# Spreading a background gather: fewer steps in the latents' first mixer, more in the last third of the first expert pass

## The chip, the cores and the metric

The kernel runs on one core of one Trainium2 chip. The metric is the device time of one execution in microseconds. The core has five engines that matter here: TensorE (PE, with weight loads as PEld), VectorE (DVE), ScalarE (ACT), GpSimd (POOL), and SyncE (SP), which issues most transfers. [...]

## The reference

Two layers of a diffusion backbone over 512 latent tokens (width 1024), with 256 context tokens beside them. Each layer is a mixer (windowed attention with context keys, pooling, a gated chunk mixer, joined by gates and an output projection) and then a retrieval of single-neuron experts. The context is updated only in the first layer. The part that the change touches is the expert retrieval:

```python
def peer_ffn(h, w_q, subkeys, u_tab, v_tab):          # one block of 128 tokens at a time
    q = (xb @ w_q).reshape(PEER_BLOCK, PEER_HEADS, 2, PEER_HALF)
    s = jnp.einsum("thpd,hpkd->thpk", q, subkeys)
    sv, si = lax.top_k(s, PEER_TOPK)
    ...                                                 # 16 of the 256 sums, for each of 8 heads
    experts = jnp.take_along_axis(cand_e, top_pos, axis=-1)
    gate = jax.nn.softmax(top_s, axis=-1)
    act = jax.nn.gelu(jnp.einsum("td,thkd->thk", xb, u_tab[experts]))
    return jnp.einsum("thk,thkd->td", (gate * act), v_tab[experts])

for layer in range(2):
    x = x + gt1 * merge_branches(...)                   # mixer of the latents
    if not last: xc = xc + cgt1 * merge_branches(...)   # mixer of the context
    x = x + gt2 * peer_ffn(modulate(x), ...)
    if not last: xc = xc + cgt2 * peer_ffn(modulate(xc), ...)
return rms_norm(x, g_final)
```

Every token has 128 experts (8 heads of 16) out of 16384, each with a row of 1024 numbers in the table u and one in the table v.

## The kernel before, in words

**Order of the work.** Context mixer of layer 0; latents' mixer of layer 0 (`mixer(0, xT, ...)`); expert pass of layer 0 (`peer(0, ...)`); mixer and expert pass of layer 1; final norm. The context's own expert retrieval has no time of its own: it runs in the background of the others.

**Latents' experts, dense.** For the 512 latents `peer` multiplies by every expert. The first pass goes through 128 tiles of table u (24 matmuls of 128x512 each, `activations`, L942 takes the gelu), the second through 128 tiles of table v (L1083 to L1085). In the first pass of layer 0, 96 tiles (`spilled`) write their activations to memory, the last 32, the last third as it is called here, are kept on the chip (`kept`). Beside the first 96 tiles runs a second background job, `front`, which finds the latents' own experts and builds their gate matrix, mostly on DVE.

**Weights.** Each weight tile is loaded by SP into `wraw`, cast by ACT to its high half (`whi`, L189), and DVE takes the difference (`wlo`, L190). `Weights.take` hands out a tile and prepares the next ones.

**Context's experts, by gathering.** The 256 context tokens are two blocks of 128. `gather` handles one expert per token at a time: POOL issues an indirect DMA that fetches 128 rows of 4 KB (`rows`, L801), one for each token, into one of four buffers (`NG4 = 4`). With table u DVE multiplies the rows by the tokens and sums (L818, followed by a read of the accumulator); with table v it adds the weighted rows to `hN` (L821 for the first, L823 for the others). After the 128 steps with u, ACT takes the gelu (L828). Two blocks and two tables make 4 × 128 steps; 6 empty steps stand before them. Gathers are issued two steps ahead of their use. DVE's gather instructions keep the program's order.

**Pace.** `Background` holds the jobs. A job has a rate and a credit; every `Weights.take` outside a background step calls `tick`, which adds the rate to the credit and runs one step for each whole unit:

```python
for job in list(self.jobs):
    job[2] += job[1]
    while job[2] >= 1.0 and job in self.jobs:
        job[2] -= 1.0
        self.step(job)
```

The gathering job is created by `gather_experts`, which the mixer calls (as `clear`) after its first branch. From there on the mixer takes 1 weight tile for the keys, 4 for the queries and 16 for the pool branch, interleaved with attention; then `faster` is called, and 16 tiles of the attention branch and 8 of the output projection follow. In the attention branch the products go from DVE (L501) to POOL, which adds them to `mg` (L502), and then to ACT and DVE, which split the sum into halves (`mr`, L214 and L215). In the output projection DVE adds to the stream (L674).

In `peer` the four numbers of `rates` pace the job: the first from the start of the first pass, the second from tile 40 on, the third in the 32 kept tiles; in the second pass the rate is what is left over `P - rates[3]`, which is 128 + 8 tiles. What is left after that is drained at the start of layer 1's mixer (`second_context`), where the sums are turned on PE and added to the context (L880, L884). Within `peer` POOL's instructions stay in the program's order.

Of the kernel before, what the change touches and what calls it, by code (L numbers as in the profile page):

```python
# [19 lines left out]
P = 128  # L20
# [62 lines left out]
def tile_backbone(ctx: ExitStack, tc: tile.TileContext, A, out):  # L83
# [5 lines left out]
    bg = Background()  # L89
# [709 lines left out]
    def rows(pool_, table, idx, tag="g4"):  # L799
        g = pool_.tile([P, D], F32, name="g4", tag=tag, bufs=NG4)  # L800
        pool.indirect_dma_start(out=g, out_offset=None, in_=A[table], in_offset=bass.IndirectOffsetOnAxis(ap=idx, axis=0))  # L801
        return g

    def gather(blocks, wait):
        lag = NG4 - 2
        for _ in range(wait):
            yield
        for b in blocks:
            hN, dots, gate = (b[k] for k in ("hN", "dots", "gate"))
            for table in ("u", "vf"):  # L810
                got = [rows(g4[0], table, b["idx"][:, s:s + 1]) for s in range(lag)]
                for s in range(SLOTS):
                    if s + lag < SLOTS:
                        got.append(rows(g4[0], table, b["idx"][:, s + lag:s + lag + 1]))
                    g = got.pop(0)
                    w = gate[:, s:s + 1]
                    if table == "u":
                        ins = dve.tensor_tensor_reduce(out=g, in0=g, in1=hN, op0=ALU.mult, op1=ALU.add, scale=1.0, scalar=0.0,  # L818
                                                 accum_out=dots[:, s:s + 1])
                    elif s == 0:  # L820
                        ins = dve.tensor_scalar(hN, g, w, None, op0=ALU.mult)  # L821
                    else:
                        ins = dve.scalar_tensor_tensor(hN, g, w, hN, op0=ALU.mult, op1=ALU.add)  # L823
                    if bg.in_order:
                        tc.keep_in_program_order(ins)
                    yield
                if table == "u":
                    act.activation(dots, dots, AF.Gelu_apprx_tanh)  # L828
                    dve.tensor_tensor(gate, dots, gate, op=ALU.mult)
# [293 lines left out]
    cblocks = []  # L1123
# [57 lines left out]
    jobs = []  # L1181
# [4 lines left out]
    def gather_experts():  # L1186
        bg.drain(jobs.pop())
        right.close()
        g4[0] = ctx.enter_context(tc.tile_pool(name="g4", bufs=1, side="right"))
        jobs.append(bg.add(gather(cblocks, 6), 2.2, 4 * P + 6))  # L1190

    def faster(pl, ps):
        jobs[0][1] = 2.0

    r = mixer(0, xT, rx[0], True, mps, start=find_experts, clear=gather_experts, after_attention=faster)
    eh.close()
    with tc.manual_schedule(engines={mybir.EngineType.Pool}):
        r = peer(0, r, (1.8, 1.4, 1.8, -8))

    kv = ExitStack()  # L1200

# [29 lines left out]
    with tc.tile_pool(name="mps", bufs=3, space=PSUM) as mps:  # L1231
        r = mixer(1, xT, r, True, mps, start=second_context, settle=context_done, after_attention=all_mods)
    with tc.manual_schedule(engines={mybir.EngineType.Pool}):
        r = peer(1, r, (0, 1.0, 1.5, 4))
# [82 lines left out]
```

## Time and profile before

| | us |
|---|---|
| median of three executions | 4099.12 |
| lowest and highest | 4096.03, 4104.95 |
| the profiled execution, its own time | 4101.82 |
| its span, first to last instruction | 4100.0 |

| engine | busy us | share of the span |
|---|---|---|
| PE | 3906.6 | 95% |
| DVE | 3146.7 | 77% |
| ACT | 1498.7 | 37% |
| POOL | 1183.0 | 29% |

How to read the lines of the profile that are shown below. The page gives the span, each engine's busy time, share and instruction count, and the span in 40 equal slices, with each slice's busy share in tenths (9 is 90% or more). A table of stretches has one line per stretch: its start and end in us from the start of the span, its length, then busy time and instruction count of each engine (PE, PEld, DVE, ACT, POOL), the mean granted clock of PE, the busy share of the 16 DMA engines, and GB/s. If it is restricted to one line of the kernel, only the engine of that line is named. A line of the waits names who waited for whom, the total in us, the number of times, and the longest. A line of the timeline gives start and duration in us, engine, line, operation, output and inputs with their shapes, and in brackets how long the engine had been idle and what ended that.

### The profile page before, as it was taken

What the parts mean: (1) busy time and instruction counts of PE and PEld (TensorE: products, weight loads), DVE (VectorE), ACT (ScalarE), POOL (GpSimd) and SP (SyncE); (2) the same over time, 40 slices, a digit from 0 to 9 for tenths busy, and PEclk for the clock granted to TensorE, in tenths of its full rate; (3) what the DMA queues carried; (4) which work ended last, traced back from release to release, by engine and by line L of the source; (5) the groups of instructions that cost most, each with busy time, mean ns of one, the idle gap of its engine ahead of it and who ended that gap; (6) DMA issues with size and microseconds to landing.
All of it is one profiled execution on the core that took longest, in us unless ns stands there. A gap on an engine that the chain in (4) does not pass through costs nothing. (4 is left out here: it accounts for less than half of the span.)

```text
span 4100.0 us, 59061 instructions
## 1 busy us (share of the span) xinstructions
PE 3906.6 (95%) x21737; PEld 3391.9 (83%) x21737; DVE 3146.7 (77%) x6154; ACT 1498.7 (37%) x2320; POOL 1183.0 (29%) x942
## 2 busy tenths in 40 slices
PE   7999898899999999999999979999999999999998
PEld 5788776678778888788888867777889999999998
DVE  4569876799998876677778875645889986788887
ACT  3553343323344433222222233443234443333333
POOL 1111244411643324343333331110002224423331
PEclk9999999899999999999999989999999999999999
DMA  7753456655998998889999854323348999989996
GB/s 282 260 172 111 147 173 212 226 189 184 325 317 309 318 308 275 296 299 358 350 344 358 318 173 140 119 89 105 118 153 295 334 332 323 341 312 353 364 358 224
DMA packets 366099, 1051.86 MB, mean 257 GB/s; under 512 B 38384, under 2 KB 131312, under 8 KB 361200
## 3 DMA queue, kind: packets, MB, share of 16 engines
q1 hardware_dynamic: 170928, 544.18, 37.6%
q0 software_dynamic: 110592, 402.70, 28.5%
q10 hardware_dynamic: 84288, 101.20, 7.0%
q8 instruction: 170, 2.79, 0.3%
q14 instruction: 121, 0.99, 0.1%
HBM read 943.61 MB, written 104.33 MB: 256 GB/s over the span
## 5 line engine op out<-in xcount | busy, mean ns | idle before, releaser
L189 ACT CAST whi<-wraw 128x1024 fp32r<-128x1024 f32 (+2 forms) x756 | 752.6, 997 | 1672.2 <-issue 596.0
L190 DVE TENSOR_TENSOR wlo<-wraw,whi 128x1024 fp32r<-128x1024 f32 (+2 forms) x756 | 876.3, 1161 | 571.1 <-ACT whi L189 465.4
L801 POOL DMA_INDIRECT g<-in_u_dram,idx x384 | 500.9, 1304 | 1228.4 <-DVE dots L818 816.7
L801 POOL DMA_INDIRECT g<-in_v_dram,idx x384 | 511.8, 1333 | 913.3 <-DVE hN L823 845.5
L220 PE MATMUL pa<-h,whi 128*128 128x512 f32 (+1 forms) x2016 | 744.0, 369 | 2.5 <-ACT a L942 2.5
L1083 PE MATMUL acc<-ah,whi 128*128 128x512 f32 (+1 forms) x2048 | 740.4, 363 | 5.6 <-ACT ah L214 5.6
L1085 PE MATMUL acc<-ah,wlo 128*128 128x512 f32 (+1 forms) x2048 | 741.5, 362 | 0.0
L1084 PE MATMUL acc<-al,whi 128*128 128x512 f32 (+1 forms) x2048 | 741.4, 362 | 0.0
L221 PE MATMUL pa<-h,whi 128*128 128x512 f32 (+1 forms) x2016 | 734.4, 364 | 0.0
L818 DVE CUSTOM_DVE_ANT_0 g<-g,hN 128x1024 f32<-128x1024 f32 x384 | 466.2, 1236 | 50.5 <-DMA g<-in_u_dram,idx 50.4
L823 DVE SCALAR_TENSOR_TENSOR hN<-g,gate,hN 128x1024 f32<-128x1024 f32 x381 | 487.2, 1279 | 13.4 <-DMA g<-in_v_dram,idx 12.9
L223 PE MATMUL pa<-h,wlo 128*128 128x512 f32 (+1 forms) x2016 | 450.2, 364 | 2.9 <-DVE wlo L190 2.9
L1083 PEld LDWEIGHTS acc<-ah,whi 128*128 128x128 f32 x2048 | 384.7, 188 | 47.2 <-ACT ah L214 7.2
L1084 PEld LDWEIGHTS acc<-al,whi 128*128 128x128 f32 x2048 | 385.1, 188 | 40.4
L1085 PEld LDWEIGHTS acc<-ah,wlo 128*128 128x128 f32 x2048 | 385.0, 188 | 40.2
L220 PEld LDWEIGHTS pa<-h,whi 128*128 128x128 f32 x2016 | 381.1, 189 | 40.9 <-ACT a L942 2.8
L221 PEld LDWEIGHTS pa<-h,whi 128*128 128x128 f32 x2016 | 380.8, 189 | 38.2
L223 PEld LDWEIGHTS pa<-h,wlo 128*128 128x128 f32 x2016 | 368.5, 189 | 42.6 <-DVE wlo L190 3.2
L220 PE MATMUL pj<-h,whi 128*128 128x512 f32 (+1 forms) x792 | 288.9, 376 | 6.6 <-DVE nx L295 3.2
L221 PE MATMUL pj<-h,whi 128*128 128x512 f32 (+1 forms) x792 | 280.9, 366 | 1.3 <-POOL h L300 0.9
L942 ACT ACTIVATE a<-pa 128x512 f32<-128x512 f32 (+1 forms) x256 | 139.3, 546 | 271.1 <-PE pa L223 203.7
L220 PEld LDWEIGHTS pj<-h,whi 128*128 128x128 f32 x792 | 154.5, 195 | 46.8 <-issue 11.5
(527 smaller groups left out, 5428.2 us busy)
## 6 DMA issues: line engine op xcount, KB each, us to landing
wraw<-in_uT_dram SPq DMA_DIRECT2D x256, 512.0 KB, 5.3
wraw<-in_v_dram SPq DMA_DIRECT2D x256, 512.0 KB, 5.9
gd<-gs ACTq DMA_DIRECT2D x28, 2048.0 KB, 13.2
wraw<-in_winT_dram SPq DMA_DIRECT2D x100, 512.0 KB, 4.2
wm<-in_wmod_dram SPq DMA_DIRECT2D x64, 512.0 KB, 5.2
g<-gd SPq DMA_DIRECT2D x16, 2048.0 KB, 10.6
wraw<-in_wq_dram SPq DMA_DIRECT2D x48, 512.0 KB, 3.9
ad<-a ACTq DMA_DIRECT2D x96, 256.0 KB, 4.9
```

The costliest lines, as they stand in the source:

```text
L189: act.copy(hi, raw)
L190: dve.tensor_tensor(lo, raw, hi.bitcast(F32), op=ALU.subtract)
L220: pe.matmul(ps, wh[i], xh[i], start=i == 0, stop=False)
L221: pe.matmul(ps, wh[i], xl[i], start=False, stop=False)
L223: pe.matmul(ps, wl[i], xh[i], start=False, stop=i == n - 1)
L801: pool.indirect_dma_start(out=g, out_offset=None, in_=A[table], in_offset=bass.IndirectOffsetOnAxis(ap=idx, axis=0))
L818: ins = dve.tensor_tensor_reduce(out=g, in0=g, in1=hN, op0=ALU.mult, op1=ALU.add, scale=1.0, scalar=0.0, accum_out=dots[:, s:s + 1])
L823: ins = dve.scalar_tensor_tensor(hN, g, w, hN, op0=ALU.mult, op1=ALU.add)
L942: act.activation(a, pa[:, n_w:], AF.Gelu_apprx_tanh)
L1083: pe.matmul(acc[c], wh[:, s], ah, start=n == 0 and c % pair == 0, stop=False)
L1084: pe.matmul(acc[c], wh[:, s], al, start=False, stop=False)
L1085: pe.matmul(acc[c], wl[:, s], ah, start=False, stop=n == P - 1 and (c % pair == 1 or pair == 1 and not blocks))
```

## The change

Four rates change. In the latents' mixer of layer 0 the gathering job starts at 1.0 steps per weight tile, was 2.2; after attention it goes on at 1.3, was 2.0. In layer 0's expert pass the rate from tile 40 of the first pass on is 1.5, was 1.4, and in the 32 kept tiles 2.3, was 1.8. The first rate of the pass and the rule for the second pass stay. No instruction of the computation is added or removed; the same 512 steps are handed out at other places.

```diff
         g4[0] = ctx.enter_context(tc.tile_pool(name="g4", bufs=1, side="right"))
-        jobs.append(bg.add(gather(cblocks, 6), 2.2, 4 * P + 6))
+        jobs.append(bg.add(gather(cblocks, 6), 1.0, 4 * P + 6))
 
     def faster(pl, ps):
-        jobs[0][1] = 2.0
+        jobs[0][1] = 1.3
 
     r = mixer(0, xT, rx[0], True, mps, start=find_experts, clear=gather_experts, after_attention=faster)
     eh.close()
     with tc.manual_schedule(engines={mybir.EngineType.Pool}):
-        r = peer(0, r, (1.8, 1.4, 1.8, -8))
+        r = peer(0, r, (1.8, 1.5, 2.3, -8))
```

## The prediction

> **What bounds the kernel now.** I read the page first, for the bound, then the slices of its second part, for the places where TensorE (PE) is not full.
>
> ```profile
> span 4100.0 us, 59061 instructions
> PE 3906.6 (95%) x21737; PEld 3391.9 (83%) x21737; DVE 3146.7 (77%) x6154; ACT 1498.7 (37%) x2320; POOL 1183.0 (29%) x942
> PE   7999898899999999999999979999999999999998
> ```
>
> PE is the bound, so the change can only win where PE stands still or runs at a lower granted clock, and can only lose by making it do so elsewhere. A slice is 102.5 us. The eighths in slices 4 and 6 to 8 lie in the latents' first mixer, where the gathering begins. The second layer runs the same mixer with no gathering at all, which makes it the yardstick. I cut both by the code: attention, from the first pool-branch gate (L491) to the first gate of the attention branch; that branch (16 weight tiles) up to the first L674; the output projection up to the last L674. The first table is all engines, layer 0 above layer 1; the second counts gather issues (L801).
>
> ```profile
> 466.90:636.70 169.80, 150.40 (x976) 119.52 (x975) 122.20 (x211) 78.20 (x178) 68.26 (x52) 0.98 0.52 169
> 2545.80:2712.00 166.20, 152.21 (x975) 121.39 (x975) 104.49 (x183) 79.25 (x179) 19.32 (x11) 0.97 0.36 117
> 636.70:735.50 98.80, 75.46 (x292) 58.29 (x292) 61.54 (x94) 22.31 (x32) 53.45 (x38) 0.90 0.70 230
> 2712.00:2779.20 67.20, 67.20 (x293) 54.50 (x292) 27.38 (x34) 23.58 (x32) 9.76 (x6) 1.00 0.31 102
> 735.50:773.40 37.90, 37.90 (x168) 30.99 (x167) 33.33 (x44) 9.71 (x12) 20.44 (x15) 1.00 0.69 234
> 2779.20:2817.10 37.90, 37.90 (x168) 30.99 (x167) 14.05 (x17) 9.70 (x12) 4.42 (x3) 1.00 0.12 42
> ...
> 636.70:735.50 98.80, 45.30 (x32) 0.90 0.70 230
> ```
>
> Read the first figure after the window, then PE's busy time, then the clock (third from the end). The attention branch alone is 31.6 us longer with 32 gathers beside it (98.80 against 67.20): PE idles 23.3 us, and the same matmuls take 8.3 us more at a clock of 0.90. Attention differs by 3.6 us, the output projection by nothing. The waits of that branch say how (the last line is layer 1):
>
> ```profile
> ACT mr L214 <- POOL mg L502: 45.6, 6, 10.9
> DVE g L818 <- DMA g<-in_u_dram,idx: 32.3, 6, 7.1
> PE pj L223 <- DVE wlo L190: 14.5, 5, 5.8
> PE pw__7295 L220 <- ACT mr L214: 6.8, 1, 6.8
> ...
> ACT mr L214 <- POOL mg L502: 17.1, 6, 2.9
> ```
>
> One turn of the branch in order of time:
>
> ```profile
> 654.80 1.23 DVE L818 CUSTOM_DVE_ANT_0 g<-g,hN 128x1024 f32<-128x1024 f32 x1 [5.27 <-DMA g<-in_u_dram,idx]
> 656.30 1.17 POOL L801 DMA_INDIRECT g<-in_u_dram,idx  x1 [4.60 <-DVE dots L818]
> 662.33 0.94 POOL L801 DMA_INDIRECT g<-in_u_dram,idx  x1 [0.30 <-issue]
> 663.29 1.31 POOL L502 TENSOR_TENSOR mg<-mg,mt 128x512 f32<-128x512 f32 x1
> 664.63 0.62 ACT L214 CAST mr<-mg 128x512 fp32r<-128x512 f32 x1 [8.83 <-POOL mg L502]
> 666.71 1.23 DVE L818 CUSTOM_DVE_ANT_0 g<-g,hN 128x1024 f32<-128x1024 f32 x1 [4.30 <-DMA g<-in_u_dram,idx]
> ```
>
> It is a ring. A dot frees a gather buffer; POOL issues four gathers (656.30 to 663.27); only then comes the branch's add (mg), for which ACT stands 8.83 us with the next weight cast queued behind; DVE meanwhile stands before a dot whose rows have not landed, with the low half of the weights (wlo) behind it, and PE waits for wlo. A turn takes 11.9 us (654.80 to 666.71) where PE needs 67.2/8 = 8.4.
>
> **The change part by part.** A step of the gathering is one gather of 128 rows, its issue on POOL, its 0.5 MB and one DVE pass; a tick comes with each weight tile. Nothing is removed; 42 steps move. Credits worked through, with fractions carried on: after the drain of context_experts the mixer has 21 ticks (1 + 4 + 16) and then 24 (16 + 8). Before: 21 × 2.2 and 24 × 2.0, so 46 + 48 = 94 steps; after: 21 × 1.0 and 24 × 1.3, so 21 + 31 = 52. Tiles 2 to 40 of the first pass: 39 × 1.8, 70 and 70. Tiles 41 to 95: 55 × 1.4 = 77, then 55 × 1.5, 82. The last third: 32 × 1.8, 58, then 32 × 2.3 and the carry, 74. Left for the second pass: 219, then 240 of 518; at 1/136 of that per tile its 128 tiles do 206, then 226, so 13, then 14 are left for the drain in layer 1's mixer. (42 fewer in the mixer = 5 + 16 + 20 + 1.)
>
> *Attention branch*: 4 steps a turn become 2.6 (five turns of 3, three of 2). Ring scaled: POOL's four issues took 6.97 us, 1.74 each, so a turn of 3 is 10.2 and one of 2 is 8.4: 76 us in all. The floor is layer 1's 67.2. I take the middle, 72: −26.8. Outer end: if DVE still stands for a landing in every turn of 3 and these keep 11.9 us, 84.7, that is −14.1; the other end −31.6. *Attention*: 46 steps to 21, between 0 and −3.6; I take −2. *Output projection*: 0, covered by PE at 37.90 of 37.90 already.
>
> The first pass, the second pass and the drain:
>
> ```profile
> 800.90:1152.60 351.70, 335.85 (x1700) 273.94 (x1699) 331.53 (x1120) 113.47 (x155) 113.18 (x70) 0.99 0.71 244
> 1152.60:1513.40 360.80, 360.80 (x2149) 296.99 (x2149) 301.17 (x375) 148.02 (x219) 130.74 (x81) 1.00 0.92 311
> 1513.40:1675.30 161.90, 161.90 (x715) 133.73 (x713) 98.25 (x120) 50.07 (x61) 67.19 (x53) 1.00 0.81 275
> 1857.00:2357.00 500.00, 500.00 (x2207) 414.04 (x2206) 399.14 (x465) 144.90 (x185) 169.82 (x150) 1.00 0.94 344
> 3740.00:3980.00 240.00, 240.00 (x1387) 240.00 (x1386) 199.93 (x237) 85.60 (x116) 75.88 (x64) 1.00 0.98 365
> ...
> q0 software_dynamic: 21530, 78.38, 43.6%
> ...
> 2399.00:2426.50 27.50, 15.34 (x12) 0.90 0.79 262
> ...
> 2426.51 1.09 PE L880 MATMUL ga<-ident,hN 128*128 128x128 f32 x8 [2.92 <-DVE hN L823]
> ...
> 1572.04 1.23 DVE L190 TENSOR_TENSOR wlo<-wraw,whi 128x1024 fp32r<-128x1024 f32 x1 [1.93 <-ACT whi L189]
> 1574.33 1.22 DVE L818 CUSTOM_DVE_ANT_0 g<-g,hN 128x1024 f32<-128x1024 f32 x1
> 1577.48 1.22 DVE L190 TENSOR_TENSOR wlo<-wraw,whi 128x1024 fp32r<-128x1024 f32 x1 [1.92 <-ACT whi L189]
> 1518.25 2.60 DVE L823 SCALAR_TENSOR_TENSOR hN<-g,gate,hN 128x1024 f32<-128x1024 f32 x2
> 1519.80 1.86 POOL L801 DMA_INDIRECT g<-in_v_dram,idx  x1 [3.97 <-DVE hN L823]
> 1525.60 1.32 DVE L823 SCALAR_TENSOR_TENSOR hN<-g,gate,hN 128x1024 f32<-128x1024 f32 x1
> ```
>
> *Tiles 2 to 40* (800.90 to 1152.60): same count, but DVE is nearly full (20.2 us free of 351.7) and PE idles 15.9. The job now starts 42 steps earlier in its list, so the change from table u to v, with its gelu, falls out of this stretch. Between −8 and +3; I take −1.
> *Tiles 41 to 95*: 5 steps more, 1.30 us of DVE each (2.60 for two): 6.5 us, in 59.6 us that DVE has free (360.80 less 301.17), under a PE that never waits. Where DVE has no room the whole 6.5 shows; 0 to +6.5, I take +1.
> *Last third*: 2.3 steps a tile of 5.44 us (wlo at 1572.04 and 1577.48). DVE: 1.14 + 2.3 × 1.30 = 4.1 of 5.44. The buffers: a dot may run only when the gather that took the buffer of the dot four before it has landed. Caught up at full speed, that ring took 7.35 us (1518.25 to 1525.60, the fourth dot after), 1.84 a step, against 5.44/2.3 = 2.37. It fits, with a fifth to spare. 0 to +10 (2.5 us a step), I take +0.5.
> *Second pass*: 0.154 steps a tile more. DVE gains 0.2 us a tile; it has 1.1 free (100.9 of 500 over 92 tiles). A gather is 0.52 MB (78.38 over 150), so 344 GB/s become 359. The layer 1 row, 365 GB/s with PE 240.00 of 240.00, covers it: 0. By "DMA: Bandwidth & Descriptors" of the Trainium skill (Where 436 GB/s comes from) a core's HBM side binds at about 358 GB/s, which speaks against the change. By that page this stretch would be 500 × 359/358, so 1.4 us longer, and the sum 1.4 us worse. The 365 of layer 1 does not bear it out.
> *Drain*: one step more. Twelve (x12) took 27.5 us with PE's transposes waiting for the last: +2 (0 to +2.3).
>
> Sum: −26.8 − 2 − 1 + 1 + 0.5 + 0 + 2 = −26.3. The profiled execution took 4101.82 us (span 4100.0), 2.7 above the median 4099.12; its sum is 4075.5, against the median 4072.8. I predict 4073.
>
> **The rivals.** *A: the ring stays in the attention branch* (84.7 us): 12.7 us less is won, 4086. For it: POOL still has up to three gathers before mg. Against: the output projection ran 12 steps in 37.9 us (POOL x15 there, three of them not gathers) with PE full, 3.2 us a step; 20.8 steps in 67.2 us are the same 3.2.
> *B, the other side: the gather ring becomes the bound of the last third.* DVE is in order, so a late landing holds wlo and then PE. It begins above 2.37 us a step, and the kernel is slower than before above 2.37 + 26.3/74 = 2.73. At the mixer's 11.9/4 = 2.98, 74 steps take 220 us against 174: +46 − 26 = 4119. For it: this row of POOL beside DVE, an issue of 0.94 us while DVE is idle and 1.68 while a dot runs:
>
> ```profile
> 1574.68 1.68 POOL L801 DMA_INDIRECT g<-in_u_dram,idx  x1 [2.50 <-DVE dots L818]
> 1576.67 0.94 POOL L801 DMA_INDIRECT g<-in_u_dram,idx  x1 [0.30 <-issue]
> ```
>
> Against: the 7.35 us above already hold an issue of 1.86. "SBUF — State Buffer" of the Trainium skill (SBUF: two separate sides) says why that could be: a DVE instruction with two SBUF inputs keeps a GpSimd operation that reads SBUF off the shared ports for its whole length. The two rows agree with it.
> *C: DVE's full stretches cost it all*: +6.5 in tiles 41 to 95 and +3 before: 4073 + 9.5 = 4082.
> *D: no gain*, the branch's 31.6 us being layer 0's own and not the gathering's: 4099 + 2.5 = 4102. Against: 45.6 us of ACT waiting behind POOL, 17.1 in layer 1.
>
> **How the numbers follow.** Forecast 0.64 (own range 4064 to 4080), A 0.16, C 0.10, B 0.06, D 0.04. The range runs from both ends of the good case (−31.6 − 3.6 − 2: 4062) to past A (4090). This kernel's measurement can tell about 0.2%, 8 us, so faster means below 4091. The forecast, C and nearly all of A: 0.88; same 0.05 (D and the rest of A); slower 0.07 (B and a little).
>
> **What would show it.** Right: the attention branch at 67 to 77 us with a clock near 1.00, ACT's wait for mg near layer 1's; 69 to 74 gathers in the last third with PE full; the second pass near 359 GB/s with PE full; 13 dots in the drain. Wrong: PE waiting for wlo between 1450 and 1650 us, DVE waiting for landings there, a turn still near 11.9 us, or PE idle in tiles 41 to 95.

## The result, and the profile after

The changed kernel takes 4058.93 us (median of four, 4053.57 to 4063.84), the kernel before 4097.89 beside it: a ratio of 0.9902, 95% interval 0.9884 to 0.9919, so 39 us less. The same kernel again, beside the last experiments (e14), gave 0.9904 (0.9889 to 0.9920). I had predicted 4073 and a range of 4062 to 4090: the direction was right, the size was not, and the time lies below the range.

The page of the changed kernel, its first lines:

```profile
span 4058.9 us, 59067 instructions
PE 3900.2 (96%) x21737; PEld 3389.4 (84%) x21737; DVE 3150.7 (78%) x6154; ACT 1501.7 (37%) x2321; POOL 1144.5 (28%) x942
PE   7999999899999999999999979999999999999998
```

The same matmuls are there. Counted from 0, the eights of slices 4 and 6 have become nines; slice 7, in which the mixer ends and the pass begins, still shows an 8. (The prediction's "6 to 8" took one slice too many: slice 8 was a nine before.) The profiled execution took 4060.67 us, 41.2 less than that of before. The latents' first mixer, cut at the same instructions as before (attention, attention branch, output projection; then the gathers alone, POOL):

```profile
462.60:623.30 160.70, 150.13 (x981) 119.16 (x980) 89.46 (x160) 78.18 (x179) 33.84 (x28) 1.00 0.32 97
623.30:690.50 67.20, 67.20 (x292) 54.48 (x291) 55.91 (x75) 23.59 (x32) 34.30 (x25) 1.00 0.76 250
690.50:728.30 37.80, 37.80 (x168) 30.93 (x166) 27.58 (x34) 9.70 (x12) 16.61 (x12) 1.00 0.50 167
...
462.60:623.30 160.70, 16.15 (x17) 1.00 0.32 97
623.30:690.50 67.20, 24.56 (x19) 1.00 0.76 250
```

The attention branch went from 98.80 to 67.20 us, exactly layer 1's time, with 19 gathers still beside it and the clock at 1.00. Attention went from 169.80 to 160.70, and that is below layer 1's 166.20, which I had used as its floor. These two make −40.7 of the −41.2. The waits of the attention branch, and one turn of it:

```profile
POOL g L801 <- DVE dots L818: 22.9, 15, 7.5
ACT mr L214 <- POOL mg L502: 17.1, 6, 2.9
ACT whi L189 <- PE pb L221: 10.2, 8, 1.3
...
655.08 1.21 DVE L818 CUSTOM_DVE_ANT_0 g<-g,hN 128x1024 f32<-128x1024 f32 x1
660.15 1.60 POOL L502 TENSOR_TENSOR mg<-mg,mt 128x512 f32<-128x512 f32 x1 [0.66 <-DVE mt L501]
661.78 0.62 ACT L214 CAST mr<-mg 128x512 fp32r<-128x512 f32 x1 [2.83 <-POOL mg L502]
663.37 1.21 DVE L818 CUSTOM_DVE_ANT_0 g<-g,hN 128x1024 f32<-128x1024 f32 x1
```

ACT's wait for the add is 17.1 us in all, layer 1's figure to the digit; no wait of DVE for a landing and none of PE is left in the list. A turn is 8.3 us (655.08 to 663.37), PE's own time.

The expert pass, in the stretches of before (tiles 1 to 40, 41 to 96, last third), the second pass, and the four tiles at its start:

```profile
756.30:1115.00 358.70, 342.17 (x1720) 279.74 (x1718) 334.40 (x1158) 116.37 (x156) 88.19 (x72) 0.98 0.70 242
1115.00:1474.20 359.20, 359.20 (x2143) 295.87 (x2142) 305.91 (x386) 145.45 (x219) 133.11 (x87) 1.00 0.93 320
1474.20:1633.20 159.00, 158.95 (x702) 131.28 (x700) 116.29 (x113) 49.44 (x62) 86.91 (x66) 1.00 0.88 312
1817.60:2317.60 500.00, 500.00 (x2208) 414.15 (x2207) 416.57 (x497) 145.98 (x185) 187.59 (x164) 1.00 0.97 359
1634.30:1665.20 30.90, 25.50 (x96) 20.16 (x97) 18.78 (x29) 5.42 (x7) 9.19 (x7) 0.89 0.99 385
```

The three stretches of the first pass add to 876.9 us, before to 874.4. The second pass runs at the 359 GB/s that were worked out, with PE 500.00 of 500.00. That is a little more than the 358 GB/s that the Trainium skill ("DMA: Bandwidth & Descriptors", "Where 436 GB/s comes from") gives as a core's limit to HBM. By that figure PE would have had to wait.

In the last third PE is full too, but DVE now waits for landings there, 36.8 us in all (the first two lines), where it waited 1.3 us in the kernel before (the last two):

```profile
DVE hN L823 <- DMA g<-in_v_dram,idx: 22.2, 23, 1.9
DVE g L818 <- DMA g<-in_u_dram,idx: 14.6, 7, 3.9
...
DVE hN L823 <- DMA g<-in_v_dram,idx: 1.1, 1, 1.1
DVE g L818 <- DMA g<-in_u_dram,idx: 0.2, 1, 0.2
```

### The profile page after: what moved, and what is told of

It reads as the page before. It is cut to its first block, busy times and chain, and to the rows that moved or that the text cites. A ratio compares the mean times of both kernels' runs of the same rounds, so it can differ in the third digit from the quotient of the medians.

```text
span 4058.9 us, 59067 instructions
## 1 busy us (share of the span) xinstructions
PE 3900.2 (96%) x21737; PEld 3389.4 (84%) x21737; DVE 3150.7 (78%) x6154; ACT 1501.7 (37%) x2321; POOL 1144.5 (28%) x942
## 5 line engine op out<-in xcount | busy, mean ns | idle before, releaser
L801 POOL DMA_INDIRECT g<-in_u_dram,idx x384 | 492.3, 1282 | 1275.2 <-DVE dots L818 849.0
L801 POOL DMA_INDIRECT g<-in_v_dram,idx x384 | 483.1, 1258 | 830.7 <-DVE hN L823 761.6
L220 PE MATMUL pj<-h,whi 128*128 128x512 f32 (+1 forms) x792 | 284.8, 372 | 4.5 <-DVE nx L295 1.5
L221 PE MATMUL pj<-h,whi 128*128 128x512 f32 (+1 forms) x792 | 276.2, 361 | 0.7 <-DVE h L303 0.4
```

The source lines that it names most:

```text
L220: pe.matmul(ps, wh[i], xh[i], start=i == 0, stop=False)
L221: pe.matmul(ps, wh[i], xl[i], start=False, stop=False)
```

## The experiments

The reason to be tested: the gain lies in the mixer alone, in two separate places, and the pass carries the moved steps for nothing. The rivals: the pass gave a part; or the branch suffers from a backlog that attention hands on.

**Which rates do it.** Four kernels, each with a part of the change, on one chip beside the kernel before at 4090.90:

```diff
 e1: gather(...) rate 1.0, faster 1.3, peer (1.8, 1.4, 1.8, -8)
 e2: gather(...) rate 2.2, faster 2.0, peer (1.8, 1.5, 2.3, -8)
 e3: gather(...) rate 1.0, faster 2.0, peer (1.8, 1.4, 1.8, -8)
 e4: gather(...) rate 2.2, faster 1.3, peer (1.8, 1.4, 1.8, -8)
```

> Only the two rates of the latents' mixer change (1.0 and 1.3); the expert pass keeps 1.8, 1.4 and 1.8, so the second pass takes the 20 or so steps that are left over, 1.92 a tile. Theory (all of the gain is in the mixer, attention and its last branch together): attention 161 us, attention branch 67, total 37 to 41 us below the kernel before, the same as the whole change within 4 us. Rival 1 (the pass gave part of it): total only 20 to 30 us below. Rival 2 (the second pass is near its limit of transfers and would not take 1.92 a tile): PE idle in the second pass, total less than 30 below.

> Only the rates of the expert pass change (1.5 in the second stretch, 2.3 in the last third); the mixer keeps 2.2 and 2.0. Theory: mixer as before (attention 170, branch 99 us), total within 4 us of before, since PE does not wait in those stretches of the pass. Rival 1 (the pass gives part of the gain): 8 us or more below before. Rival 2 (the full stretches of DVE cost): 4 to 9 us above.

> Only the first mixer rate changes (1.0 for the 21 tiles of keys, queries and pool branch); the attention branch and output projection keep 2.0, the pass its old rates. Theory (two separate costs): attention 161 us instead of 170, attention branch still 95 to 99, total 8 to 11 us below before. Rival (one cost: a backlog that attention hands to the branch): the branch falls by 10 us or more as well and the total by over 18.

> Only the second mixer rate changes (1.3 for the attention branch and the output projection); attention keeps 2.2, the pass its old rates. Theory (two separate costs): attention 170 us, attention branch 67 to 70, total 28 to 32 us below before. Rival (backlog from attention): branch still over 80 us, total less than 20 below.

| kernel | median us | ratio to before, 95% | attention us | attention branch us |
|---|---|---|---|---|
| e1, mixer only | 4058.87 | 0.9922 (0.9905 to 0.9938) | 160.6 | 67.2 |
| e2, pass only | 4091.58 | 1.0002 (0.9992 to 1.0013) | 171.5 | 95.2 |
| e3, attention only | 4074.59 | 0.9957 (0.9941 to 0.9974) | 160.6 | 96.4 |
| e4, branch only | 4063.65 | 0.9929 (0.9909 to 0.9949) | 170.6 | 67.2 |

Each mixer rate moves its own stretch and leaves the other alone, so there is no backlog. The rates of the pass give nothing that can be measured in the total. e1's 32 us are less than the 37 expected, but its interval (25 to 39 us) overlaps that of the whole change. By medians e3 and e4 give 16 and 27 (8 to 11 and 28 to 32 were expected), together 44 against the 32 of e1; e3's profile, besides its 9 us in attention, has tiles 1 to 40 at 346.8 us where e2, with the same first rate, has 352.6: such stretches differ by some us between kernels. In e1 the second pass has to take 1.92 steps a tile:

```profile
1800.00:2300.00 500.00, 499.86 (x2204) 413.37 (x2203) 433.26 (x538) 148.80 (x186) 240.09 (x181) 1.00 1.00 381
```

381 GB/s with PE still full, so 359 was not yet a wall. The DMA engines are busy all of that time (share 1.00), so a wall may be close above 381.

**What attention's floor is.** Both kernels have the whole change. e6 sets both mixer rates to 0; e7 stops layer 1's own background job (`mod_rest`, which loads 512 KB at a time and makes DVE passes for the modulation's columns) until attention is over:

```diff
 e6: gather(...) rate 0.0, faster 0.0, peer (1.8, 1.5, 2.3, -8)
 e7: -        jobs.append(bg.add(mod_rest(g4[0], "g4", NG4, silu, 1), 1.5))
     +        jobs.append(bg.add(mod_rest(g4[0], "g4", NG4, silu, 1), 0.0))
```

> The whole change, but with both mixer rates 0: no gathering at all in the mixer, 52 more steps in the pass, about 2.15 a tile in the second pass. Theory (attention's floor is below layer 1's 164 to 166 us): attention 157 to 160 us, branch 67. In the second pass 2.15 steps a tile would be some 395 GB/s by the sizes: if that is more than it takes, PE idles there (10 to 40 us) and the total comes out above the changed kernel's. Rival (attention's floor is layer 1's, the 160.7 us of the changed kernel were luck): attention 164 to 166.

> The whole change, and in layer 1's mixer the background job with the modulation's columns (32 DVE passes of 1.3 us, rate 1.5) gets rate 0, so that all of it is done at once after attention. Theory (layer 1's mixer was no empty yardstick, that job costs its attention 4 to 6 us): layer 1's attention falls from 164 to 158 to 161 us; after it PE stands some 40 us while the job is done, so the total is 25 to 40 us above the changed kernel. Rival (attention differs between the layers for another reason): layer 1's attention stays at 163 to 166.

Attention of layer 0 in e6; its second pass; attention of layer 1 in e7 and the branch after it; and the passes of that job (L162, each counted with its read) in layer 1's attention in the kernel before:

```profile
458.80:616.30 157.50, 149.73 (x982) 119.07 (x981) 68.74 (x126) 77.16 (x179) 18.96 (x11) 1.00 0.13 46
1810.70:2310.70 500.00, 479.25 (x2045) 386.02 (x2045) 420.58 (x537) 137.86 (x171) 243.65 (x184) 0.99 0.98 371
...
2498.70:2657.40 158.70, 151.08 (x981) 120.66 (x980) 71.76 (x131) 78.27 (x179) 18.95 (x11) 0.99 0.14 47
2657.40:2759.40 102.00, 70.68 (x292) 56.29 (x292) 65.18 (x96) 23.57 (x32) 11.05 (x6) 0.85 0.60 210
...
2545.80:2712.00 166.20, 35.50 (x54) 0.97 0.36 117
```

Freed of its job, layer 1's attention takes 158.70 us; freed of the gathers, layer 0's takes 157.50. So the yardstick was not empty: 27 passes, 35.50 us of DVE, lay in it. The third busy time in those lines, DVE's, puts the five attentions in order:

| attention of | DVE busy us | attention us |
|---|---|---|
| layer 0, kernel before | 122.20 | 169.8 |
| layer 1, kernel before | 104.49 | 166.2 |
| layer 0, changed kernel | 89.46 | 160.7 |
| layer 1, e7 | 71.76 | 158.7 |
| layer 0, e6 | 68.74 | 157.5 |

The transfers of the five come in the same order (169, 117, 97, 47 and 46 GB/s), so they are a rival. A run from the next group, e13, tells the two apart. It gathers as the kernel before does (42 gathers in attention against 41), but DVE multiplies only half of each row. Its attention:

```profile
462.20:627.30 165.10, 152.00 (x979) 121.43 (x978) 100.37 (x211) 77.46 (x179) 61.38 (x53) 0.98 0.53 175
```

With 175 GB/s and 100.37 us of DVE it takes 165.1 us in its one run, where the five kernels with the same rate and whole passes (before, e2, e4, e5, e10) take 169.3 to 171.5. So DVE's passes count, and not the transfers alone. PE's longest wait in attention shows the way: it waits for ACT's exponential of the scores (L587), which waits for DVE's maximum (L585, L586). That wait is 10.9 us in layer 0 of the kernel before, 7.5 in the changed kernel and 4.8 in e6. DVE has room on average in all of these kernels; that single passes delay attention's own reductions is my reading of it. Busy time is not the whole rule: e12 below has 161.5 us with 86.42 of DVE, and e9, which fixes POOL's order, 188.6 with 121.89.

e7 pays back more than it gains, in the branch (102.00 instead of 67.20): 4079.80 in one run. e6 pays in the second pass: 184 gathers in 500 us are 2.72 us a step, PE loses 20.8 of these 500 us (DMA share 0.98), and the kernel took 4108.72 in one run. What leaves the mixer is not free without limit.

**Why a turn took 12 us.** Three kernels from the kernel before, all rates kept, each changing one suspected link: e5 moves POOL's add to DVE, e9 makes POOL keep the program's order through the whole mixer, e10 issues gathers one step earlier. Two vary the load: the changed kernel with 1.65 in the branch (e11), and the kernel before with half of DVE's pass (e13, which leaves the other half of those sums out).

```diff
 e5: -  (pool if br == 1 or o < 6 else dve).tensor_tensor(mg[:, o], mg[:, o], t, op=ALU.add)
     +  (pool if br == 1 else dve).tensor_tensor(mg[:, o], mg[:, o], t, op=ALU.add)
 e9: +  with tc.manual_schedule(engines={mybir.EngineType.Pool}):
            r = mixer(0, xT, rx[0], True, mps, ...)
 e10: -  lag = NG4 - 2
      +  lag = NG4 - 1
 e11: -  jobs[0][1] = 1.3
      +  jobs[0][1] = 1.65
 e13: -  dve.tensor_tensor_reduce(out=g, in0=g, in1=hN, ...)
      +  dve.tensor_tensor_reduce(out=g[:, :512], in0=g[:, :512], in1=hN[:, :512], ...)
```

> All rates as before; only the attention branch's add into mg runs on DVE for all 8 outputs (before: 6 on POOL, 2 on DVE), so it no longer stands in POOL's queue behind the gathers. Theory (the ring goes through POOL's add: gathers, add, ACT's split, weight cast): the branch falls from 97 us to 67 to 78 with its 32 gathers still in it, ACT no longer waits for POOL, total 20 to 30 us below before. Rival 1 (the ring is the gather's own: DVE stands for landings, POOL's add is only late by it): branch stays at 92 us or more. Rival 2 (DVE is short of time): the branch gets longer.

> All rates as before; in the latents' first mixer POOL's instructions keep the program's order, as they do in the expert pass already. In the kernel before the first dot of a turn waited for the third gather that POOL issued in that turn (issued at 660.03, dot at 666.71), so the buffers had come out of step with the program. Theory (that order makes the ring as long as 3 us a step): branch falls to 67 to 80 us with 32 gathers in it. Rival (four steps a turn are too many for DVE's queue in whatever order): branch stays over 90 us.

> All rates as before; gathers are issued three steps ahead of their use instead of two, with the same four buffers. Theory (DVE stands for landings because gathers are issued too late): DVE's waits for landings in the branch fall below 15 us (32.3 before) and the branch below 90. Rival (the four buffers are the limit, each comes free only with a dot): branch within 4 us of 97.

> The whole change, with 1.65 instead of 1.3 in the attention branch and the output projection, 3.3 steps a turn of 8.4 us. Theory (a limit: a ring of some 3 us a step, so 2.8 steps fit into a turn): branch between 72 and 82 us, in proportion. Rival (the loss needs four steps a turn, below it PE stays full): branch under 70 us.

> The kernel before with all its rates; with table u DVE multiplies only the first 512 of a row's 1024 numbers (the other half of those sums is left out), about 0.6 us less of DVE in each step; gathers and buffers are untouched. Theory (a turn is a ring of landings and buffers, in which four passes of 1.15 us stand one behind another): branch falls by that share only, 8 turns of 4 times 0.6 us at the most, to 78 to 92 us. Rival 1 (DVE's own time is short, 61.5 us busy of 98.8): branch near 67 to 72. Rival 2 (only landings count): branch stays at 94 to 99.

The attention branch in each, in that order, and after e5's line its waits and the ends of one of its turns:

```profile
631.50:728.70 97.20, 75.77 (x292) 59.45 (x291) 64.39 (x101) 22.77 (x32) 43.14 (x32) 0.91 0.70 233
ACT mr L214 <- DVE mg L502: 54.7, 8, 10.2
DVE g L818 <- DMA g<-in_u_dram,idx: 28.9, 6, 6.3
PE pj L223 <- DVE wlo L190: 16.1, 5, 4.5
649.33 1.23 DVE L818 CUSTOM_DVE_ANT_0 g<-g,hN 128x1024 f32<-128x1024 f32 x1 [4.82 <-DMA g<-in_u_dram,idx]
656.86 0.72 DVE L502 TENSOR_TENSOR mg<-mg,mt 128x512 f32<-128x512 f32 x1
661.21 1.22 DVE L818 CUSTOM_DVE_ANT_0 g<-g,hN 128x1024 f32<-128x1024 f32 x1 [3.63 <-DMA g<-in_u_dram,idx]
...
650.10:737.80 87.70, 73.40 (x296) 56.73 (x296) 61.49 (x94) 21.87 (x32) 48.20 (x38) 0.96 0.78 258
632.30:727.70 95.40, 74.65 (x292) 58.02 (x291) 61.71 (x95) 22.35 (x32) 51.50 (x38) 0.91 0.71 238
624.50:697.50 73.00, 67.64 (x292) 54.40 (x291) 57.02 (x84) 22.73 (x32) 40.60 (x30) 1.00 0.78 266
627.30:712.30 85.00, 72.96 (x292) 57.08 (x291) 46.17 (x94) 22.30 (x32) 42.04 (x37) 0.92 0.75 265
```

e5 is a miss of my theory. Without POOL's add the branch is as long as with it (the same rates in the branch gave 95.2 to 98.8 in the kernel before, e2, e3 and e10), and the total is the same too (0.9999, 0.9988 to 1.0010). ACT now waits just as long, 54.7 us, for the add on DVE. A turn of e5 takes 11.88 us (649.33 to 661.21), as before; DVE has done the add by 657.6 and then stands 3.63 us for a landing. So POOL's add, for which ACT stood 45.6 us, is no link that the long turn needs.

e10: 95.40, no effect (4086.88 in one run), so issuing earlier without more buffers does not help. e9: 87.70, between both expectations. POOL's order has a part in it: DVE's wait for landings fell from 32.3 us to 10.5. But attention took 188.6 us there, and the kernel 4109.48 in one run. e13 leaves transfers and buffers alone: 85.00, with DVE's wait for landings still 32.3 us (4063.13 in one run). So DVE's passes are a part, but not all.

What is left, by exclusion, is the ring of four buffers, in which landings and DVE's passes stand one behind another: a dot that must wait for its rows holds what stands behind it on DVE, wlo too (before: 32.3 us of DVE before such dots, 14.5 us of PE before wlo). No run had another number of buffers, so this is argued and not shown. The number of steps a turn shows where the loss begins: 2.6 a turn 67.2 us, 3.3 a turn 73.0 (e11, 4059.53 in one run), 4 a turn 95 to 99. How a turn of 12 us divides between landing, order and passes was not settled.

**Where the last third would have failed.** The changed kernel with 3.2 in the last third:

```diff
-        r = peer(0, r, (1.8, 1.5, 2.3, -8))
+        r = peer(0, r, (1.8, 1.5, 3.2, -8))
```

> The whole change with 3.2 instead of 2.3 steps a tile in the last third: 1.70 us a step, below the 1.84 to 2.1 that the ring of four buffers took when it ran freely. Theory (the ring's limit lies there, and PE's weight tiles ahead cover little of it): DVE waits for landings in the last third, PE idles 5 to 25 us in it, total 5 to 20 us above the changed kernel, fewer steps in the second pass. Rival (the ring can go faster or DVE's wait is covered): PE idles under 2 us, total within 4 us of the changed kernel.

Last third, its gathers over 151.8 us of it, and its waits:

```profile
1466.80:1674.50 207.70, 175.18 (x696) 138.68 (x696) 142.50 (x158) 47.26 (x61) 123.91 (x89) 0.93 0.85 298
...
1504.60:1656.40 151.80, 91.62 (x66) 0.92 0.85 297
...
ACT whi L189 <- DMA wraw<-in_uT_dram: 124.0, 21, 8.9
PE pa L223 <- DVE wlo L190: 28.3, 11, 5.4
```

The stretch is 48.7 us longer than the changed kernel's 159.0. PE idles 32.5 us in it, where 5 to 25 were expected. The kernel is slower than before, 1.0054 (1.0035 to 1.0072), 58 us above the changed kernel on the same chip (e14), where 5 to 20 were expected. 66 steps in 151.8 us are 2.30 us a step. So beside weight tiles the gathers come no faster than about one in 2.30 us, not the 1.84 that I read from one quick stretch, and the change, which asks for one in 2.37, has a few per cent to spare. Past the limit DVE's wlo comes late, the raw tile's buffer comes free late, and the next weight load starts late: SP's weight loads wait 187.1 us for wlo in this stretch, 139.3 in the changed kernel's.

**A version from this.** The changed kernel, with layer 1's job at 0.6 in attention, 1.25 in the branch, and drained before the output projection:

```diff
-        jobs.append(bg.add(mod_rest(g4[0], "g4", NG4, silu, 1), 1.5))
+        jobs.append(bg.add(mod_rest(g4[0], "g4", NG4, silu, 1), 0.6))
...
+    def more_mods(pl, ps):
+        jobs[0][1] = 1.25
```

> The whole change, and layer 1's own background job (32 DVE passes for the modulation's columns) goes 0.6 per weight tile in attention instead of 1.5, then 1.25 in the attention branch, and is drained before the output projection. Theory (DVE is what attention lacks, in both layers): layer 1's attention 159 to 162 us instead of 164 to 166, its attention branch stays at 67 (DVE had 27 of 67 us to do), total 3 to 6 us below the changed kernel. Rival (the branch pays it back): layer 1's branch 70 us or more, total the same as the changed kernel.

> The whole change once more, beside the others on the same chip: 33 to 41 us below the kernel before, attention 160 to 162 us, attention branch 67, last third and second pass with PE full.

```profile
2501.90:2663.40 161.50, 150.97 (x979) 120.26 (x980) 86.42 (x153) 79.34 (x179) 18.92 (x11) 0.99 0.25 85
2663.40:2730.60 67.20, 67.20 (x292) 54.50 (x292) 53.30 (x69) 23.61 (x32) 9.90 (x6) 1.00 0.62 209
```

Layer 1's attention falls to 161.50 us and its branch stays at 67.20, so the stretch behaves as expected. The total does not show it: 4054.46 against 4054.63 for the changed kernel on the same chip (0.9900, 0.9886 to 0.9915, and 0.9904, 0.9889 to 0.9920, to the kernel before). Some 3 us are below what these runs can tell. In e14 the changed kernel's own stretches came again as they were: attention 160.60, attention branch 67.20.

## Why the prediction was right and wrong

*The bound and the place*: right. PE is the bound, the gain is PE's idle time and lost clock in the mixer, and the output projection did not move.

*The attention branch*, −26.8 taken, −14.1 to −31.6 allowed: it was −31.6. The step was right in kind, and the size was the good end. Scaling POOL's share of a turn put 76 us on 2.6 steps; the runs show that at this number nothing of the loss is left (67.2 at 2.6, 73.0 at 3.3). And the link that I drew through POOL's add was wrong: e5 took it off POOL and the turn stayed. Rivals A (84.7 us) and D (no gain) did not come; e4 alone brings the branch to 67.2.

*Attention*, −2 taken and −3.6 the most allowed: it was −9.1, and −9.2 in e3. This is the step that failed. "The same mixer with no gathering at all, which makes it the yardstick" overlooked that layer 1's mixer carries a job of its own; the code says so, and DVE's 104.49 us in the quoted row were there to be compared with 122.20. The low end of 4062 was built on that floor, and the 5.5 us beyond −3.6 are more than the 3 us by which the time lies below it. Of the 14 us between 4073 and the time, attention holds 7.1 and its branch 4.8.

That the time fell below the range was in part luck all the same. The changed kernel's profiled execution was also 4.3 us ahead at the first gate of layer 0's mixer and 2.0 us shorter in layer 1's attention, where the change has no part, or only its first ticks; without these 6 us the time would have been inside the range. The low end also took −2 for everything else without saying from where; tiles 2 to 40 alone were allowed −8.

*The first pass*: −1, +1 and +0.5 taken, the whole pass +2.5 in the profiled executions. Single stretches moved more (tiles 1 to 40 +7.0, which my +3 did not allow, the other two −1.6 and −2.9). That is no effect of the change: in e14, the same kernel, tiles 1 to 40 took 350.8 us, against 351.7 before. Rival C did not come.

*The last third*: PE full, but 66 gathers issued by its end where I had said 69 to 74, and DVE waiting 36.8 us for landings, which I had named as a sign of being wrong. PE did not have to wait there all the same (158.95 of 159.00 us busy). "With a fifth to spare" was too sure: e8 puts the limit at 2.30 us a step against 2.37. Rival B's mechanism is real, and the change stops just short of it.

*The second pass*: 359 GB/s as worked out, PE full. The 358 GB/s of the Trainium skill ("DMA: Bandwidth & Descriptors", "Where 436 GB/s comes from") are not borne out as a limit here, neither at 359 nor at 381 GB/s. The first four tiles took 30.9 us instead of 28.2, +2.7 that I had at nothing. This goes with the last third's rate: of the pass's first 28.2 us PE was busy 24.7 to 24.8 in four kernels with 1.8 there (before, e1, e3, e4), 22.7 to 23.6 in four with 2.3 (changed, e14, e2, e6) and 16.5 in e8.

*The drain*: one step more and +2 taken, 13 dots expected. It was 14 instead of 12, and from PE's transposes of the first block (L880) to those of the second it took 3.3 us more. The stretch behind it, up to the first pool gate of layer 1, was 4.9 us shorter; the reason stays open.

## What to carry to other kernels

A stretch without the suspected work is a floor only if it carries no other background work: compare the busy time of the engine in question in both before taking one for the yardstick. Move background steps out of a stretch where the gathers must come faster than their few buffers let them, and count in the target stretch what the same gathers take beside that stretch's work, not what it took once in a quick moment. A long wait behind a queue need not be the cause: take the queued work away and see whether the wait only changes its name.

## What the hardware showed that was not expected

The core took 381 GB/s over 500 us with PE busy 499.86 of them (e1); I had counted on 365. With PE losing time, the same four buffers gave a different rate beside each kind of work: one step in about 3 us in the attention branch at four gathers a turn (2.7 with POOL's order fixed, e9), one in 2.30 beside first-pass weight tiles (e8), and one in 2.72 beside second-pass tiles (e6). Whether e6 was held by the buffers or by the transfers, with a DMA share of 0.98, no run tells.
